# The recurrence's elementwise tiles, made pair by pair in the projections of a hybrid decoder layer and kept in HBM

## The chip, the core and the metric

The kernel runs on one core of a Trainium2 chip. TensorE (PE) multiplies matrices, VectorE (DVE), ScalarE (ACT) and GpSimd (POOL) work elementwise, SyncE (SP) issues most of the DMAs and ACT a few. Each engine works through its own instructions in the order in which the program lists them. The metric is the device time of one execution in microseconds (us).

## The reference

One inference step of a two-layer decoder for a prompt of 1024 tokens and eight samples of eight tokens, model width 1024. Each layer is a mixer, a cross-attention over 256 memory tokens and a squared-ReLU MLP. The mixer of layer 0 is a convolution module, that of layer 1 is RWKV-7 time mixing, which is what changes here:

```python
xr, xw, xk, xv, xa, xg = (h + xx * mix[i] for i in range(6))
r, k, v = xr @ w_r, xk @ w_k, xv @ w_v
w_pre = w0 + tanh(xw @ w1) @ w2
decay = exp(-exp(-softplus(-w_pre) - 0.5))
a = sigmoid(a0 + (xa @ a1) @ a2)
g = sigmoid(xg @ g1) @ g2
kk = k * k_k;  kk = kk / max(sqrt(sum(kk * kk)), 1e-12)      # per head of 64
k = k * (1 + (a - 1) * k_a)
# per token:  s = s * decay + (s @ -kk) (kk * a)^T + v k^T ;  y = s @ r
y = standardize(y) * lnx_g + lnx_b
bonus = sum(r * k * r_k) * v                                  # per head
out = ((y + bonus) * g) @ w_o
```

## The kernel before

Everything is kept channel by token: 128 channels on the partitions, eight blocks of channels (a block holds two heads of 64, so it is a pair of heads; `m` counts the blocks). The tokens are cut into two parts, and each part has a stream of its own: stream A works on part 0 (512 tokens), stream B on part 1 (512 tokens and the 64 sample tokens). Tiles of A have an A in their names (`A_d`, `hAA`, `xA`), those of B a B.

Each stream runs the same stages: convolution, attention, MLP, then in layer 1 the projections (`projections`), the recurrence (`scan`), its output product (`mixer_out`), attention, MLP. A function `pace` takes steps from the two streams in turn, by costs that the steps yield, and stream B's recurrence waits for A's. A list scheduler then fixes the order of every engine's instructions when the program is built. So while A is in its recurrence, what else PE can do is what the order places there of stream B, and the reverse.

Large products are made of three fp32r matmuls for each pair of 128 rows (L142 to L144, in `prod`; the rounded operand and its rest are made by `split`, L96 and L97).

`projections` makes r, k, v (`project`, 24 weight tiles) and the low-rank w, a and g (`hidden`, `lora`) and writes them with `store` into `scr`, one array in HBM for each block, with six slots. `scan` goes over chunks of 64 tokens: eight of part 0, and for part 1 the sample tokens and eight chunks. Its steps for a chunk are generators that `together` runs side by side for three neighbouring chunks:

- `prep` loads the chunk of all eight blocks from `scr` (16 DMAs, L1151), makes the running decay sum (L1171), its exponentials, the scaled r, k, kk and kk*a (L1166 to L1203), the norms of kk with four matmuls (L1208), and the bonus term (L1256 to L1258), all on tiles of 128x512, and between them the products of the chunk (L1224 to L1253);
- `invert` inverts the chunk's triangular matrices of 64x64, mostly on DVE (L1276 to L1322, then PE and DVE in turn);
- `step` carries the state S from chunk to chunk (L1381 to L1408), `step_samples` does the samples;
- `finish` normalizes y and applies lnx_g, lnx_b, the bonus and g on POOL (L1467 to L1471).

The MLP's square on POOL is L711, the time mixing's interpolations are L782 and L783, the attention's spill to HBM is `xa`, and `low` keeps the low halves of the projection weights between the two parts.

## Time and profile before

| | |
|---|---|
| runs of the kernel, us | 3828.97, 3836.46, 3836.49 (median 3836.46) |
| the profiled execution: its time, us | 3837.42 |
| its span, first to last instruction, us | 3835.7 |
| PE busy, us | 3623.9 (94% of the span) |
| DVE busy, us | 2351.6 (61%) |
| ACT, POOL busy, us | 1610.0 (42%), 660.7 (17%) |
| mean granted clock of PE | 0.955 |
| DMA, mean | 119 GB/s |

The span leaves out 1.7 us of the profiled execution's time. Busy shares are means over stages that differ, so the prediction reads them stretch by stretch. The granted clock is a mean over a stretch of PE's two levels, 2.4 GHz (1.00) and 1.2 GHz (0.50).

### The profile page before, as it was taken

What the parts mean: (1) busy time and instruction counts of PE and PEld (TensorE: products, weight loads), DVE (VectorE), ACT (ScalarE), POOL (GpSimd) and SP (SyncE); (2) the same over time, 40 slices, a digit from 0 to 9 for tenths busy, and PEclk for the clock granted to TensorE, in tenths of its full rate; (3) what the DMA queues carried; (4) which work ended last, traced back from release to release, by engine and by line L of the source; (5) the groups of instructions that cost most, each with busy time, mean ns of one, the idle gap of its engine ahead of it and who ended that gap; (6) DMA issues with size and microseconds to landing.
All of it is one profiled execution on the core that took longest, in us unless ns stands there. A gap on an engine that the chain in (4) does not pass through costs nothing.

```text
span 3835.7 us, 75763 instructions
## 1 busy us (share of the span) xinstructions
PE 3623.9 (94%) x30906; PEld 3369.6 (88%) x30906; DVE 2351.6 (61%) x4479; ACT 1610.0 (42%) x3190; POOL 660.7 (17%) x704
## 2 busy tenths in 40 slices
PE   8989979999999999999979998879999999989998
PEld 7767769999999999998768898758799999989998
DVE  7889974646545554437896444778955546553334
ACT  3223253435433354544555654444543435332222
POOL 0010031114201100002332000243330025101110
PEclk9999989999999999999979998889899999989998
DMA  6414223335422344544333784432233336322222
GB/s 226 132 53 129 80 67 106 102 114 170 153 90 83 126 151 152 159 138 112 85 88 109 232 254 146 111 93 70 54 113 120 114 120 197 121 72 83 83 83 64
DMA packets 333004, 456.03 MB, mean 119 GB/s; under 512 B 155248, under 2 KB 247664, under 8 KB 332656
## 3 DMA queue, kind: packets, MB, share of 16 engines
q1 hardware_dynamic: 305008, 424.43, 36.4%
q10 hardware_dynamic: 27648, 26.75, 2.0%
q8 instruction: 243, 3.98, 0.4%
q14 instruction: 105, 0.86, 0.1%
HBM read 369.11 MB, written 73.49 MB: 115 GB/s over the span
## 4 chain that ended last, share of the span: by engine, by line
PE 77%; DVE 11%; ACT 4%; DMA 4%; issue 2%; POOL 1%; SPq 1%; ACTq 0%; DVEq 0%; POOLq 0%
PE B_d L142 11%; PE B_d L144 11%; PE B_d L143 11%; PE A_d L142 10%; PE A_d L143 9%; PE A_d L144 9%; PE A_d L362 3%; PE B_d L362 2%; DMA scr<-t_st 1%; SPq L1151 1%; PE A_hd L810 1%; PE A_d L442 1%; PE B_sa L608 1%; DVE wt L97 1%; PE B_sa L610 1%
## 5 line engine op out<-in xcount | busy, mean ns | idle before, releaser
L97 DVE TENSOR_TENSOR wt<-raw,wt 128x1024 fp32r<-128x1024 f32 x447 | 567.3, 1272 | 476.9 <-ACT wt L96 473.0
L96 ACT CAST wt<-raw 128x1024 fp32r<-128x1024 f32 x488 | 508.5, 1047 | 502.2 <-PE B_d L144 268.6
L142 PE MATMUL B_d<-hAB,wt 128*128 128x288 f32 (+1 forms) x2240 | 673.6, 303 | 15.4 <-ACT hAB L96 6.3
L143 PE MATMUL B_d<-hBB,wt 128*128 128x288 f32 (+1 forms) x2240 | 668.5, 299 | 1.2 <-DVE hBB L97 1.1
L144 PE MATMUL B_d<-hAB,wt 128*128 128x288 f32 (+1 forms) x2240 | 666.2, 298 | 0.3 <-DVE wt L97 0.3
L142 PE MATMUL A_d<-hAA,wt 128*128 128x256 f32 x2240 | 639.1, 288 | 15.0 <-ACT hAA L96 13.6
L143 PE MATMUL A_d<-hBA,wt 128*128 128x256 f32 x2240 | 642.4, 288 | 3.4 <-DVE hBA L97 3.4
L144 PE MATMUL A_d<-hAA,wt 128*128 128x256 f32 x2240 | 632.8, 285 | 2.5 <-POOL wt L97 2.2
L142 PEld LDWEIGHTS A_d<-hAA,wt 128*128 128x128 f32 x2240 | 429.0, 192 | 25.1 <-ACT hAA L96 16.8
L142 PEld LDWEIGHTS B_d<-hAB,wt 128*128 128x128 f32 x2240 | 425.4, 191 | 24.5 <-ACT hAB L96 7.5
L143 PEld LDWEIGHTS A_d<-hBA,wt 128*128 128x128 f32 x2240 | 430.2, 192 | 14.3 <-DVE hBA L97 5.6
L144 PEld LDWEIGHTS A_d<-hAA,wt 128*128 128x128 f32 x2240 | 428.6, 192 | 7.3 <-POOL wt L97 2.6
L143 PEld LDWEIGHTS B_d<-hBB,wt 128*128 128x128 f32 x2240 | 427.2, 191 | 6.5 <-DVE hBB L97 3.7
L711 POOL TENSOR_TENSOR t_sg<-t_ev 128x256 f32<-128x256 f32 (+1 forms) x256 | 185.5, 725 | 1418.2 <-ACT t_ev L709 1329.3
L144 PEld LDWEIGHTS B_d<-hAB,wt 128*128 128x128 f32 x2240 | 426.1, 190 | 2.3 <-issue 0.7
L142 PE MATMUL B_d<-u,wt 128*128 128x288 f32 x1024 | 307.1, 301 | 0.0
L144 PE MATMUL B_d<-u,wt 128*128 128x288 f32 x1024 | 303.3, 299 | 0.0
L143 PE MATMUL B_d<-u,wt 128*128 128x288 f32 x1024 | 303.3, 298 | 0.0
L143 PE MATMUL A_d<-u,wt 128*128 128x256 f32 x1024 | 288.2, 282 | 0.0
L144 PE MATMUL A_d<-u,wt 128*128 128x256 f32 x1024 | 288.2, 282 | 0.0
L142 PE MATMUL A_d<-u,wt 128*128 128x256 f32 x1024 | 287.4, 282 | 0.0
L97 DVE TENSOR_TENSOR u<-t_sg,u 128x256 fp32r<-128x256 f32 (+1 forms) x256 | 130.4, 510 | 149.9 <-ACT u L96 149.6
(401 smaller groups left out, 7068.8 us busy)
## 6 DMA issues: line engine op xcount, KB each, us to landing
raw<-in_mlp_up_dram SPq DMA_DIRECT2D x128, 512.0 KB, 3.6
raw<-in_mlp_dn_dram SPq DMA_DIRECT2D x128, 512.0 KB, 3.6
raw<-in_rw_w_dram SPq DMA_DIRECT2D x64, 512.0 KB, 4.2
ld<-scr SPq DMA_DIRECT2D x136, 128.0 KB, 3.2
wf<-in_w_in_dram SPq DMA_DIRECT2D x32, 512.0 KB, 4.0
raw<-in_xa_w_q_dram SPq DMA_DIRECT2D x32, 512.0 KB, 3.6
raw<-in_xa_w_o_dram SPq DMA_DIRECT2D x32, 512.0 KB, 3.6
raw<-in_ck_dram SPq DMA_DIRECT2D x32, 512.0 KB, 3.6
```

The source lines that it names most:

```text
L96: self.nc.scalar.copy(hi, src)
L97: (engine or self.nc.vector).tensor_tensor(lo, src, hi.bitcast(F32), SUB)
L142: self.nc.tensor.matmul(out, lhsT=wh, rhs=mh, start=(i == 0), stop=False)
L143: self.nc.tensor.matmul(out, lhsT=wh, rhs=ml, start=False, stop=False)
L144: self.nc.tensor.matmul(out, lhsT=wl, rhs=mh, start=False, stop=(i == last))
L362: nc.tensor.matmul(ps[:, :n], lhsT=wt[:, 0, k * P:k * P + P], rhs=h[:, k, t0:t0 + n], start=(k == 0), stop=(k == NC8 - 1))
L442: nc.tensor.matmul(ps[hs], lhsT=dg[:, q, h], rhs=two[h][:, 2 * q:2 * q + 512], start=(q == 0), stop=(q == pairs - 1))
L608: nc.tensor.matmul(out[:, h2], lhsT=wt.rearrange("p i t -> p (i t)"), rhs=moving[:, 0], start=start, stop=stop)
L610: nc.tensor.matmul(out[:64, h2], lhsT=wt[:, 0], rhs=moving[:, 1], start=False, stop=False)
L711: nc.gpsimd.tensor_mul(sg[:, :n], r[:, :n], r[:, :n])
L810: nc.tensor.matmul(ps[:, :n], lhsT=w1[:, m:m + P], rhs=hc[:, :n], start=(c == 0), stop=(c == NC8 - 1))
L1151: nc.sync.dma_start(out=dst[..., m * 64:m * 64 + 64], in_=scr[part][m][:, slots, t0:t0 + 64])
```

## The change

Most elementwise work of `prep` and `finish` goes into a new generator `staged` in `projections`. It works through the eight blocks, and each block in pieces of tokens: two of 256 in part 0 (16 pieces in all), three of 192 in part 1 (24 pieces). For a piece it loads the six slots of `scr` into one tile `ld` (it has one buffer), `stage` computes on it, in place, and the seven results are written to a new array `tls` in HBM; the next piece's load goes into the same `ld`. The squared norms and the chunk-end decays are kept in SBUF (`sums`, `ends`).

`prep` now loads four ready tiles and v, and copies the norms; `finish` loads two ready tiles, multiplies once and adds once. The recurrence's inversions, products and state step are as before. The `a` path's `hidden` moves to the first projection and its `lora` beside the third, and a block's pieces are issued in the third projection once its inputs are there, the last blocks behind it.

```diff
+    tls = [[dram.tile([P, 7, n], F32, name=f"tls{i}_{m}") for m in range(NC8)] for i, (_, n, _) in enumerate(PARTS)]
+    sums = [const.tile([P, NC8, n], F32, name=f"sums{i}") for i, n in enumerate((8, 9))]
+    ends = [const.tile([P, NC8, n], F32, name=f"ends{i}") for i, n in enumerate((8, 16))]
...
+        half, pieces = (192, (0, 3, 6)) if part else (256, (0, 4))
+        ld = hp.tile([P, 7, half], F32, name="ld")
...
+        def stage(m, c0):
+            nch = half // 64
+            tail_in = c0 + nch > 8
+            e_runs = cuts[1:] if tail_in else cuts[:1]
+            w, r, ag, k, v, g, bo = (ld[:, i] for i in range(7))
+            nc.scalar.activation(kk, k, AF.Copy, scale=col("k_k", m))
+            nc.scalar.activation(t1, k, AF.Square, scale=col("k_k", m))
+            ps = s.bank()
+            for i in range(nch):
+                for hs in (slice(0, 64), slice(64, P)):
+                    nc.tensor.matmul(ps[hs, i:i + 1], lhsT=t1[hs, 64 * i:64 * i + 64], rhs=bones[hs, hs][:, :1],
+                                     start=True, stop=True)
+            nc.vector.tensor_scalar_max(sums[part][:, m, c0:c0 + nch], ps[:, :nch], L2_MIN)
+            nc.vector.tensor_tensor_scan(out=w, data0=last_rst if tail_in else rst, data1=w, initial=0.0, op0=MUL, op1=ADD)
+            for e, l in zip(e_runs, runs(w, c0)):
+                nc.scalar.activation(e[:, :, 1:], l, AF.Exp, scale=-DECAY)
+            nc.scalar.activation(w, w, AF.Exp, scale=DECAY)
+            yield .3
+            nc.scalar.activation(t1, ag, AF.Identity, scale=col("k_a", m), bias=less[:, m:m + 1])
+            nc.vector.scalar_tensor_tensor(out=ag, in0=kk, scalar=-1.0, in1=ag, op0=MUL, op1=MUL)
+            nc.vector.scalar_tensor_tensor(out=t1, in0=t1, scalar=1.0, in1=k, op0=ADD, op1=MUL)
+            nc.vector.scalar_tensor_tensor(out=bo, in0=r, scalar=col("r_k", m), in1=t1, op0=MUL, op1=MUL)
+            nc.gpsimd.tensor_tensor(ag, ag, w, MUL)
+            nc.gpsimd.tensor_tensor(k, t1, w, MUL)
+            for i, (e, l, x1, x2, x3) in enumerate(zip(e_runs, (64, DSEQ), runs(r, c0), runs(kk, c0), runs(w, c0))):
+                e0, e1 = (8, 16) if i else (c0, min(8, c0 + nch))
+                nc.gpsimd.tensor_copy(ends[part][:, m, e0:e1], e[:, :, l])
+                nc.gpsimd.tensor_tensor(x1, x1, e[:, :, 1:], MUL)
+                nc.vector.tensor_tensor(x3, x2, e[:, :, :l], MUL)
+            yield .3
+            ps = s.bank()
+            nc.tensor.matmul(ps[:, :half], lhsT=bones, rhs=bo, start=True, stop=True)
+            nc.vector.tensor_tensor(bo, v, ps[:, :half], MUL)
+            nc.vector.scalar_tensor_tensor(out=bo, in0=bo, scalar=col("lnx_b", m), in1=g, op0=ADD, op1=MUL)
+            nc.scalar.activation(g, g, AF.Copy, scale=col("lnx_g", m))
+            yield .3
+        def staged():
+            old = None
+            for m in range(NC8):
+                yield 0
+                for c0 in pieces:
+                    if old is not None:
+                        nc.sync.dma_start(out=old, in_=ld)
+                    ts = slice(64 * c0, 64 * c0 + half)
+                    nc.sync.dma_start(out=ld[:, :6], in_=scr[part][m][:, :, ts])
+                    yield from stage(m, c0)
+                    old = tls[part][m][:, :, ts]
+            nc.sync.dma_start(out=old, in_=ld)
...
                         s.prod(ps[:, :n], wide(wt, h, tt))
                         t = s.small("st")
                         nc.scalar.copy(t[:, :n], ps[:, :n])
-                        store(t, m, (slot + 1) % 3, t0, n)
+                        store(t, m, (1, 3, 4)[slot], t0, n)
                         yield cost(n)
                         for side in sides:
                             yield next(side, 0)
+                    if slot == 2 and m0 and tt == tiles[-1]:
+                        for _ in range(1 + 3 * len(pieces)):
+                            yield next(tiles_of, 0)
                     if m0 == 6 and after is not None:
                         yield from mix(after, tt)
         for tt in tiles:
             yield from mix(0, tt)
-        yield from project(0, 2, hidden(1, "w", [AF.Tanh]))
-        yield from project(1, 3, hidden(5, "gh", [AF.Sigmoid, AF.Sigmoid]), lora("w", 3))
-        yield from project(2, None, hidden(4, "a", [AF.Copy]), lora("gh", 5))
+        tiles_of = staged()
+        yield from project(0, 2, hidden(1, "w", [AF.Tanh]), hidden(4, "a", [AF.Copy]))
+        yield from project(1, 3, hidden(5, "gh", [AF.Sigmoid, AF.Sigmoid]), lora("w", 0))
+        yield from project(2, None, lora("a", 2), lora("gh", 5))
         s.put()
-        yield from lora("a", 4)
+        yield from tiles_of
...
-BUF = dict(w=5, bon=2, at=2, ar=2, Aq=2, UV=2, AV=2, BK=2, v=2, pcs=3)
+BUF = dict(w=5, ld=3, at=2, Aq=2, UV=2, AV=2, BK=2, v=2, pcs=3)
...
     def load(dst, c, slots):
         part, t0 = (1, 512) if c is None else (c // 8, c % 8 * 64)
         for m in range(NC8):
-            nc.sync.dma_start(out=dst[..., m * 64:m * 64 + 64], in_=scr[part][m][:, slots, t0:t0 + 64])
+            nc.sync.dma_start(out=dst[:, m], in_=tls[part][m][:, slots, t0:t0 + 64])
     def prep(chunk):
         sam = chunk is None
         kind = "_s" if sam else "_p"
-        ld = new([P, 4, 512], "ld")
-        load(ld, chunk, slice(1, 5))
-        r, k, ws, ag = (ld[:, i] for i in range(4))
+        part, n = (1, 8) if sam else (chunk // 8, chunk % 8)
+        ld = new([P, 8, 4, 64], "ld")
+        load(ld, chunk, slice(0, 4))
+        ar, bk = ld[:, :, :2], ld[:, :, 2:]
         v = w512("v")
-        load(v, chunk, 0)
-        ar = new([P, 8, 2, 64], "ar")
-        bk = new([P, 8, 2, 64], "bk")
-        kk = w512()
-        nc.vector.tensor_tensor(v3(kk), v3(k), bvec("k_k"), MUL)
...
-        nc.vector.tensor_tensor_scan(out=L, data0=masks["rst"], data1=ws, initial=0.0, op0=MUL, op1=ADD)
...
-        nc.scalar.activation(En, L, AF.Exp, scale=DECAY)
...
-            nc.gpsimd.tensor_tensor(ar[:, :, 0], v3(kk), E[:, :, :64], MUL)
-        t1 = w512()
-        nc.vector.scalar_tensor_tensor(out=v3(t1), in0=v3(ag), scalar=-1.0, in1=bvec("k_a"), op0=ADD, op1=MUL)
-        bp = ag
-        nc.vector.scalar_tensor_tensor(out=bp, in0=kk, scalar=-1.0, in1=ag, op0=MUL, op1=MUL)
-        nc.gpsimd.tensor_tensor(bk[:, :, 0], v3(bp), v3(En), MUL)
-        km = t1
-        nc.vector.scalar_tensor_tensor(out=km, in0=t1, scalar=1.0, in1=k, op0=ADD, op1=MUL)
-        nc.gpsimd.tensor_tensor(ar[:, :, 1], v3(r), v3(E) if sam else E[:, :, 1:], MUL)
-        nc.gpsimd.tensor_tensor(bk[:, :, 1], v3(km), v3(En), MUL)
-        rk = w512()
-        t = w512()
-        nc.gpsimd.tensor_tensor(v3(t), v3(r), bvec("r_k"), MUL)
-        nc.vector.tensor_tensor(rk, t, km, MUL)
+        load(v3(v), chunk, 4)
+        pcs = ends[part][:, :, 8:] if sam else ends[part][:, :, n]
         yield
-        ss = bank("pp")
-        for q in range(4):
-            nc.tensor.matmul(ss[:, 2 * q:2 * q + 2], lhsT=sq[:, q * P:q * P + P], rhs=bones[:, ::64], start=True, stop=True)
-        d4 = d32[:, :16].rearrange("p (q c i) -> p q c i", c=2, i=2)
-        for cp, ps in heads:
-            for h, hs in heads:
-                nc.vector.tensor_scalar_max(d4[hs, :, cp], ss[ps, h:8:2].unsqueeze(2).broadcast_to([64, 4, 2]), L2_MIN)
+        d4 = d32[:, :16].rearrange("p (c i) -> p c i", i=2)
+        nc.vector.tensor_copy(d4, sums[part][:, :, n].unsqueeze(2).broadcast_to([P, 8, 2]))
...
-        sb = bank("pp")
-        nc.tensor.matmul(sb, lhsT=bones, rhs=rk, start=True, stop=True)
-        bon = w512("bon")
-        nc.vector.tensor_tensor(bon, v, sb, MUL)
-        return dict(chunk=chunk, ar=ar, at=at, Aq=Aq, UV=UV, AV=AV, BK=BK, bon=bon, pcs=pcs)
+        return dict(chunk=chunk, ar=ar, at=at, Aq=Aq, UV=UV, AV=AV, BK=BK, pcs=pcs)
...
-        gg = w512("gg")
-        load(gg, chunk, 5)
+        gb = new([P, 8, 2, 64], "gb")
+        load(gb, chunk, slice(5, 7))
         nc.gpsimd.tensor_mul(y, y, rs)
-        nc.gpsimd.tensor_tensor(v3(y), v3(y), bvec("lnx_g"), MUL)
-        nc.gpsimd.tensor_tensor(v3(y), v3(y), bvec("lnx_b"), ADD)
-        nc.gpsimd.tensor_add(y, y, w["bon"])
-        nc.gpsimd.tensor_mul(y, y, gg)
+        nc.gpsimd.tensor_mul(v3(y), v3(y), gb[:, :, 0])
+        nc.gpsimd.tensor_add(v3(y), v3(y), gb[:, :, 1])
```

Three places show what the order of the instructions becomes. The first is PE where part 0's projections end and its recurrence starts. Before, the recurrence's first rows (L1208 is the norms of a chunk, L1381 its state step) stand between stream B's MLP products (`B_d<-u,wt`):

```order
L143 MATMUL B_d<-u,wt 128x288
L1208 MATMUL p_pp<-c_bones,w 128x2 x4
L144 MATMUL B_d<-u,wt 128x288
L142 MATMUL B_d<-u,wt 128x288
L143 MATMUL B_d<-u,wt 128x288
L144 MATMUL B_d<-u,wt 128x288
L143 MATMUL B_d<-u,wt 128x288
L144 MATMUL B_d<-u,wt 128x288
L1381 MATMUL p_pz<-S,ar 64x64 x16
```

Now the pieces stand there. L912 is the eight small norm matmuls of a piece, L934 its bonus sum; the rows ahead of them are the norm of stream B's layer 1, the last of B's rows for a while. This is where piece 10 of the 16 begins:

```order
L260 MATMUL B_d<-c_ident,nv 128x128 x2
L260 MATMUL B_d<-c_ident,nv 128x32
L912 MATMUL A_d<-c_bones,t_12809 64x1 x8
L934 MATMUL A_d<-ld,c_bones 128x256
L912 MATMUL A_d<-c_bones,t_12809 64x1 x8
```

The same two rows follow each other seven times, for pieces 10 to 16, and this is where they end (L1261 is the first product of the recurrence, the next L142 the first projection product of stream B):

```order
L912 MATMUL A_d<-c_bones,t_12809 64x1 x8
L934 MATMUL A_d<-ld,c_bones 128x256
L1261 MATMUL p_pp<-ld 128x128 x2
L1414 MATMUL p_pz<-S,ld 64x64 x2
L142 MATMUL B_d<-hAB,wt 128x288 x2
```

Between the norm matmuls of neighbouring pieces 1 to 10 of part 0, 99 to 282 other matmuls stand in PE's order; between those of pieces 10 to 16 there is none. Of the 23 gaps between part 1's 24 pieces, fifteen hold 96 to 208 matmuls, and the other eight hold 12, 86, 74, 36, 56, 75, 87 and 64.

The second place is DVE at the same point. Before, stream B's projections begin (`rest`, the first DVE row of `projections` for part 1) in the middle of part 0's recurrence, between rows of a state step (L1408) and of the output (L1456):

```order
L1407 TENSOR_TENSOR S<-p_pz,S 128x512
L1322 STREAM_TRANSPOSE T_20125<-td 128x256
L1408 TENSOR_TENSOR S<-S,pcs 128x512
L725 TENSOR_TENSOR xB_169<-xB_169,B_d 128x288
L769 TENSOR_SCALAR rest<-vec 128x48
L1456 SCALAR_TENSOR_TENSOR y<-p_pz,y 128x512
```

Now that row stands behind the last row of the last piece of part 0 (L937), and with it all of stream B's mixing:

```order
L924 SCALAR_TENSOR_TENSOR ld<-ld,vec,t_12809 128x256
L931 TENSOR_TENSOR ld<-kk,ones 128x256
L935 TENSOR_TENSOR ld<-ld,A_d 128x256
L937 SCALAR_TENSOR_TENSOR ld<-ld,vec 128x256
L1309 STREAM_TRANSPOSE dt<-d_18201 128x32
L773 TENSOR_SCALAR rest<-vec 128x48
```

The third place is PE in the recurrence of part 1. Before, products of stream A (`A_d`) stand between the chunk's rows (L1235 and L1245 are transposes of `prep`, L1333 and L1342 belong to the inversion):

```order
L1333 MATMUL p_half<-td,Y_25567 32x16 x4
L1381 MATMUL p_pz<-S,ar 64x64 x3
L143 MATMUL A_d<-hBA,wt 128x256
L144 MATMUL A_d<-hAA,wt 128x256
L142 MATMUL A_d<-hAA,wt 128x256
```

Now, at the same steps of a chunk, row follows row of the recurrence:

```order
L1366 MATMUL p_half<-td,Y_26634 32x16 x32
L1272 MATMUL p_pp<-c_ident,v 128x128 x4
L1282 MATMUL p_pp<-c_ident,ld 128x128 x4
L1414 MATMUL p_pz<-S,ld 64x64 x10
L1375 MATMUL p_half<-T_29141,at 32x32 x16
L1282 MATMUL p_pp<-c_ident,ld 128x128 x4
L1288 MATMUL p_pp<-UV,Aak 64x64 x10
```

From the first row of the samples' step to the last row of part 1's recurrence, PE's order held 1008 product matmuls of stream A (L142 to L144) and now holds 112; in part 0's recurrence it held 983 of stream B and now holds 768.

## Rows read from the trace of the kernel before

**Rows 1.** The page: span, busy time of each engine, the chain that ended last.

```profile
span 3835.7 us, 75763 instructions
...
PE 3623.9 (94%) x30906; PEld 3369.6 (88%) x30906; DVE 2351.6 (61%) x4479; ACT 1610.0 (42%) x3190; POOL 660.7 (17%) x704
...
PE 77%; DVE 11%; ACT 4%; DMA 4%; issue 2%; POOL 1%; SPq 1%; ACTq 0%; DVEq 0%; POOLq 0%
```

**Rows 2.** Windows: us; busy (count) PE, PEld, DVE, ACT, POOL; PEclk, DMA, GB/s.

```profile
1340.00:1740.00 400.00, 399.77 (x3080) 396.17 (x3079) 181.25 (x335) 189.45 (x416) 28.61 (x44) 1.00 0.48 150
1740.00:2130.00 390.00, 349.76 (x4661) 300.09 (x4660) 314.93 (x700) 213.90 (x429) 116.85 (x105) 0.89 0.37 99
2130.00:2300.00 170.00, 159.73 (x1069) 147.57 (x1068) 64.88 (x132) 96.60 (x201) 6.21 (x5) 1.00 0.79 251
2300.00:2860.00 560.00, 505.70 (x6057) 435.03 (x6057) 408.08 (x855) 260.72 (x534) 162.67 (x133) 0.88 0.34 93
2500.00:2600.00 100.00, 78.80 (x871) 58.89 (x870) 84.25 (x175) 47.16 (x100) 45.25 (x34) 0.86 0.30 80
```

**Rows 3.** DMA issues of the whole kernel: count, size, median us to landing.

```profile
raw<-in_mlp_up_dram SPq DMA_DIRECT2D x128, 512.0 KB, 3.6
...
low<-wt SPq DMA_DIRECT2D x24, 512.0 KB, 3.0
...
xa<-xA SPq DMA_DIRECT2D x4, 1024.0 KB, 5.1
...
xA<-xa SPq DMA_DIRECT2D x4, 1024.0 KB, 6.1
...
xA<-xs SPq DMA_DIRECT2D x2, 1024.0 KB, 9.0
...
ld<-scr SPq DMA_DIRECT2D x136, 128.0 KB, 3.2
```

**Rows 4.** Groups by line: 256-wide DVE and POOL, table loads, a weight's split.

```profile
L711 POOL TENSOR_TENSOR t_sg<-t_ev 128x256 f32<-128x256 f32 x128 | 94.8, 741 | 591.2 <-ACT t_ev L709 504.0 <-DVE nv L252 77.6 <-DVE nt L235 3.8
...
L783 DVE SCALAR_TENSOR_TENSOR t_dl<-xA,vec,t_dl 128x256 f32<-128x256 f32 x48 | 22.4, 488 | 3.4 <-ACT t_dl L782 3.3
...
L1463 ACT ACT_TABLE_LOAD x17 | 21.8, 1283 | 0.3
...
L97 DVE TENSOR_TENSOR wt<-raw,wt 128x1024 fp32r<-128x1024 f32 x447 | 567.3, 1272 | 476.9 <-ACT wt L96 473.0
```

**Rows 5.** Groups by line: six rows of DVE in a chunk's preparation.

```profile
L1171 DVE TENSOR_TENSOR_SCAN ld<-rst,ld 128x512 f32<-128x512 f32 x17 | 26.8, 1578 | 2.2 <-DMA v<-scr 2.2
...
L1192 DVE SCALAR_TENSOR_TENSOR w<-ld,vec 128x512 f32<-128x512 f32 x17 | 17.4, 1026 | 0.0
...
L1197 DVE SCALAR_TENSOR_TENSOR w<-w,ld 128x512 f32<-128x512 f32 x17 | 15.6, 915 | 0.0
...
L1194 DVE SCALAR_TENSOR_TENSOR ld<-w,ld 128x512 f32<-128x512 f32 x17 | 15.3, 900 | 0.1
...
L1203 DVE TENSOR_TENSOR w<-w 128x512 f32<-128x512 f32 x17 | 13.6, 800 | 0.2 <-PE p_pp L1208 0.2
...
L1258 DVE TENSOR_TENSOR bon<-v,p_pp 128x512 f32<-128x512 f32 x17 | 11.5, 679 | 7.8 <-PE p_pp L1256 7.8
```

**Rows 6.** Groups by line: PE in the recurrence.

```profile
L1381 PE MATMUL p_pz<-S,ar 64*64 64x64 f32 x512 | 25.9, 247 | 1.6 <-ACT rs L1463 1.6
...
L1256 PE MATMUL p_pp<-w,c_bones 128*128 128x512 f32 x34 | 22.8, 757 | 1.4 <-ACT BK L1246 1.4
...
L1208 PE MATMUL p_pp<-c_bones,w 128*128 128x2 f32 x136 | 21.2, 274 | 1.8 <-ACT AV L1253 1.8
```

**Rows 7.** Timeline of DVE: the same step of two neighbouring chunks, part 1.

```profile
2625.60 1.04 DVE L1286 STREAM_TRANSPOSE M<-dgz 128x512 f32<-128x512 f32 x1
...
2662.68 1.08 DVE L1286 STREAM_TRANSPOSE M<-dgz 128x512 f32<-128x512 f32 x1
```

**Rows 8.** One line's instructions: duration in ns, smallest, median, largest.

```profile
L1194 DVE SCALAR_TENSOR_TENSOR ld<-w,ld x17: 654/691/1672, 1749.7 to 2748.2; 128x512 f32<-128x512 f32 x17
```

69 lines of the change are left out of this document (30 added, 39 removed).

## The prediction

> **What bounds the kernel now.** The page comes first: PE is busy for 3623.9 of 3835.7 us, and 77% of the chain that ended last lies on it [rows 1]. So what counts is where PE idles or runs at less than its full clock, and for that I read windows [rows 2]. In part 0's projections (1340 to 1740 us) PE is busy 399.8 of 400 us at clock 1.00: whatever stands beside them is hidden. In part 0's recurrence (1740 to 2130) PE idles 390 - 349.8 = 40 us, and a mean clock of 0.89 takes about 0.11 x 350 = 38 us more: a shortfall of 78 us. In the start of part 1's recurrence and its chunks (2300 to 2860) it is 560 - 505.7 = 54 us of idle time and about 0.12 x 506 = 60 us by the clock, 114 us. The stretch before it (2130 to 2300) idles 10 us. In the middle of part 1's recurrence (2500 to 2600) DVE is busy 84% and PE 79%: the chain of a chunk, mostly DVE with hand-offs to PE and ACT, sets the pace there, and 37.1 us pass from one chunk's step to the next's [rows 7].
>
> The change takes DVE and POOL work out of the two recurrences, where there is 78 + 114 = 192 us to be had at most, and puts it beside the projections. So the question is whether it is hidden there.
>
> **Part 0's tail.** The order says that it is not, for pieces 10 to 16. They stand back to back on PE with nothing between, ahead of the recurrence's first product; behind them, on DVE, stands all of stream B's mixing, so B's next products (the `hAB` row) can't be early either. SP issues load and store in turn into the one buffer `ld`: a store waits for the piece's computing, the next load for that store. So nothing overlaps, and a piece's period is the sum of three parts.
>
> The load is 6 x 256 x 4 x 128 bytes = 768 KB, the store seven slots, 896 KB. A load of 512 KB lands in 3.6 us and one of 1024 KB in 6.1; a store of 512 KB in 3.0 and one of 1024 KB in 5.1 [rows 3]. Halfway for the load, 4.9 us, and three quarters of the way for the store, 4.6. The computing's longest path is the scan (half of 1.578 us [rows 5], 0.8), two exponentials (no 256-wide Exp is in the trace; like the 0.49 us of a 256-wide row [rows 4], 1.0), and POOL's three products of 0.74 us each [rows 4] and a small copy, about 2.8. With 0.9 us for four or five hand-offs (a choice) that is 5.5 us. The period is 4.9 + 4.6 + 5.5 = 15.0 us. From piece 10 to piece 16 that is 6 x 15.0 = 90 us. Then come the last piece's computing behind its norm (3.5), its store (4.6) and the recurrence's first loads and preparation (3.2 us a load [rows 3], and their queue of 16: I take 8). The little that PE does in the tail (56 small products of 0.27 us that partly overlap, and 7 bonus products of under 0.76 [rows 6]) is counted below as added work, and I take 8 us off here. Sum **+98, taken as +100**. Bounds: with 3.6 and 3.0 us for the transfers the period is 12.1, the sum 81; with 9.0 (the slowest transfer of 1024 KB [rows 3]) and 6.1 it is 20.6, the sum 132.
>
> The page "DMA: Bandwidth & Descriptors" of the Trainium skill (section "Anatomy of one DMA") gives a DMA about 2.0 us fixed, and then bytes over 436 GB/s, for DMAs that GpSimd issues. By it, as an estimate, 1024 KB take 4.4 us, where the rows show 5.1 and 6.1, so the rows decide; its load and store would be 3.8 and 4.1 us, the period 13.4 and this term some 10 us less. It speaks against the change all the same: a chain through one buffer pays a fixed part twice for each piece.
>
> **Part 0's recurrence.** Each of eight chunks loses these DVE rows: 1578 + 1026 + 915 + 900 + 800 + 679 ns = 5.9 us [rows 5], 47 us in all of the 315 that DVE is busy there [rows 2]; POOL loses four products of about 1.4 us less the copies, and ACT three rows. PE waits there mostly on that chain, and stream B's products, now those of its projections, still fill holes. I take four fifths of the 47: **-38**. Bounds: -10, if the inversions and the state step set the pace anyway, and -70, nearly the whole shortfall of 78.
>
> **Part 1's pieces.** With 192 tokens a piece moves 576 and 672 KB: by the same rows 4.2 and 3.9 us, and 5.4 of computing, 13.5. A projection product takes 399.77 us / 3080 = 0.13 us [rows 2], so a gap of 104 matmuls in PE's order just covers a period. Fifteen gaps hold 96 to 208 and cover it, near enough. The other eight (12, 86, 74, 36, 56, 75, 87, 64, together 490) miss 8 x 104 - 490 = 342 matmuls, 44 us. I take 40 where the window before had 10 idle: +30.
>
> **Part 1's recurrence.** A chunk takes 37.1 us now, and 84% of that DVE is busy, 31.3 us [rows 2, 7]. It loses the 5.9 of rows 5. It also loses cover: stream A's products there fall from 1008 to 112, or by 100 for each of nine chunks, and with them the splitting of about four weights (1.27 us each [rows 4]) and the eviction adds, some 8 us of DVE. 17.4 us of DVE stay, and a chunk can't be faster. If it kept its busy share it would be at 21; with all idle time as before (5.8 us), at 23; and if only the six rows went, at 31. I take 26, since three neighbouring chunks still run side by side but nothing fills between. What PE does of use in it: now 0.79 x 37.1 x clock 0.86 = 25 us at full clock, less 100 x 0.13 = 13, so 12. The shortfall of a chunk is 26 - 12 = 14 us, times nine 126, where it was 114: +12, of which the end of the samples' part and the finish (two POOL products fewer of 1.2 to 1.5 us) may give back 9. With the pieces: **+33**. Bounds: at 21 us a chunk it would be 9 x 5 = 45 less, at 31 as much more; with the pieces fully covered (-10) or not, I keep -20 to +85.
>
> **PE's own work and ACT.** PE drops 136 norm products and 34 halves of bonus sums (21.2 + 22.8 us, [rows 6]), and gains 40 bonus sums of half the width and less and some 270 narrow ones, which overlap as the 64x64 ones do: **-4** (-12 to +8). ACT loads its tables 37 times more, 1.28 us each [rows 4], 47 us on an engine that is busy 189 of 400 us in the projections [rows 2]: hidden there, since the pieces' own chain has room in the long gaps. If it were not, it would add to the period of the pieces that change tables, and that lies within the bounds of the period.
>
> **Sum.** 100 - 38 + 33 - 4 = +91. The sum is made against the profiled execution, 3837.4 us, 1 us above the median of the runs: **3928 us**. With all bounds at one end it is -21 or +215.
>
> **Rivals.**
> - *The recurrences give back more than the tail costs (faster).* The work that leaves them may have delayed more than itself. One line does the same work on the same shape in 654 ns at best and 1672 at worst [rows 8], so DVE is held up by something, and POOL worked beside it. If three quarters of the 192 us go, 144, then 3837 + 100 - 144 - 4 = 3789 us. It decides from 104 us on. For it speaks that spread; against it, that inversions and state step stay, that the cover goes to 112 products, and that the median of that line, 691, is near its best. The page "SBUF — State Buffer" of the Trainium skill (section "Who interferes with whom") says that a DVE instruction with two SBUF inputs and a GpSimd one that reads SBUF lock each other out of a shared port for a whole instruction; the spread fits it, though no row here shows a lock, and in the pieces the same pairs meet again.
> - *Part 1's pieces starve as well (slower still).* If a piece takes 4 us more, as with transfers of 9 us that compete with the weights' (the window 2130 to 2300 moves 251 GB/s at a DMA share of 0.79 [rows 2]), the tail pays 6 x 4 = 24, the eight short gaps 8 x 4 = 32: 3928 + 56 = 3984 us.
> - *It cancels (no change).* PE's work is nearly the same, and if the tail is at its lower bound, 81, and the recurrences give back 77 in all, it stays at 3837. It asks for both recurrences to gain, the second without cover.
>
> **How the numbers follow.** Two runs of this kernel differ by up to 0.2% (3828.97 and 3836.49), so less than 0.2% can't be told from no change. The tail is in the order and its period rests on rows that are close, so the forecast, slower by 25 to 165 us, has 0.68; starving pieces 0.15; the gain 0.11; cancelling 0.06. That gives faster 0.11, same 0.06, slower 0.83. For 8 in 10 the range leaves out the gain and a little above: 3862 (tail 85, recurrences -60 together) to 4000 (starving, and the last 16 us of the tail's upper bound).
>
> **What would show it.** The tail: right if at the end of part 0's projections PE is nearly idle for about 90 us, with loads and stores in turn every 15 us; wrong if some product of stream B runs there, or the period is under 12. The recurrences: right if part 0's shortfall is about 40 us, and a chunk of part 1 takes some 26 us with PE idle half of it; wrong if a chunk takes over 31 or under 21. The pieces of part 1: right if PE waits at the norm of the eight with short gaps, and not of the others. The forecast falls if the recurrences give back more than 100 us together, or if PE waits in the long gaps too.

## The result, and the profile after

The changed kernel takes 4174.4 us (median of four runs, 4167.95 to 4183.58) against 3836.5: 338 us slower, ratio 1.0885 (1.0857 to 1.0912). The forecast was 3928, so the direction was right and the size missed by 246 us. The page after, with the rows that answer to [rows 1]:

```profile
span 4170.2 us, 77208 instructions
...
PE 3742.2 (90%) x31360; PEld 3452.6 (83%) x31360; DVE 2336.5 (56%) x4637; ACT 1726.0 (41%) x3424; POOL 579.8 (14%) x747
...
PE 66%; DMA 12%; DVE 10%; ACT 7%; issue 4%; POOL 1%; SPq 1%; ACTq 0%; DVEq 0%; POOLq 0%
```

PE's share of the chain that ended last fell from 77 to 66%, and DMA's rose from 4 to 12%. The windows show where. They follow the stages of [rows 2]; part 0's projections now stand in two rows, with the seven last pieces in the second (columns as in [rows 2]):

```profile
1340.00:1850.00 510.00, 495.45 (x3830) 487.08 (x3828) 254.62 (x483) 251.88 (x523) 64.67 (x90) 0.99 0.51 165
1850.00:2000.00 150.00, 43.75 (x329) 32.98 (x330) 64.09 (x159) 38.24 (x84) 20.56 (x40) 0.55 0.41 121
2000.00:2350.00 350.00, 318.56 (x4193) 265.18 (x4192) 210.06 (x536) 213.97 (x437) 31.38 (x26) 0.87 0.42 116
2350.00:2900.00 550.00, 451.31 (x3385) 423.20 (x3385) 259.45 (x566) 251.68 (x524) 81.02 (x147) 0.89 0.54 169
2900.00:3300.00 400.00, 327.81 (x4397) 257.19 (x4396) 212.30 (x512) 152.03 (x301) 51.30 (x48) 0.72 0.34 86
```

For each stage I add PE's idle time and what the clock takes, (1 - clock) x busy time, as the prediction did; in part 1, where the forecast gave one term of +33, its two parts stand apart:

| stage | shortfall before, us | after, us | more | forecast |
|---|---|---|---|---|
| part 0's projections | 0 | 20 | +20 | 0 |
| its last pieces | - | 106 + 20 = 126 | +126 | +100 |
| part 0's recurrence | 78 | 31 + 41 = 73 | -5 | -38 |
| part 1's projections | 10 | 99 + 50 = 148 | +138 | +30 |
| part 1's recurrence | 115 | 72 + 92 = 164 | +49 | +3 |

These make 328 of the 338 us. The second row of the windows is the tail, with PE busy 44 of 150 us at a clock of 0.55. The timeline there shows one piece, from the scan when its load has landed to the next piece's scan (start, duration, engine, line, what ended the idle time before):

```profile
1891.64 0.69 DVE L916 TENSOR_TENSOR_SCAN ld<-rst,ld 128x256 f32<-128x256 f32 x1 [9.80 <-DMA ld<-scr]
...
1891.70 0.51 ACT L907 ACTIVATE kk<-ld,vec 128x256 f32<-128x256 f32 x1 [9.32 <-DMA ld<-scr]
...
1892.12 0.49 ACT L908 ACTIVATE t<-ld,vec 128x256 f32<-128x256 f32 x1
...
1892.66 1.02 PE L912 MATMUL A_d<-c_bones,t 64*64 64x1 f32 x16 [11.90 <-ACT t L908]
...
1893.73 0.60 ACT L921 ACTIVATE t<-ld,less,vec 128x256 f32<-128x256 f32 x1 [0.36 <-PE A_d L912]
...
1894.36 0.42 DVE L922 SCALAR_TENSOR_TENSOR ld<-kk,ld 128x256 f32<-128x256 f32 x1 [0.47 <-ACT t L921]
...
1894.87 0.84 POOL L925 TENSOR_TENSOR ld<-ld 128x256 f32<-128x256 f32 x1 [1.70 <-DVE ld L922]
...
1895.23 0.75 DVE L924 SCALAR_TENSOR_TENSOR ld<-ld,vec,t 128x256 f32<-128x256 f32 x1
...
1895.66 0.91 POOL L926 TENSOR_TENSOR ld<-t,ld 128x256 f32<-128x256 f32 x1
...
1896.04 1.22 PE L934 MATMUL A_d<-ld,c_bones 128*128 128x256 f32 x2 [2.36 <-DVE ld L924]
...
1896.60 0.88 DVE L931 TENSOR_TENSOR ld<-kk,ones 128x256 f32<-128x256 f32 x1 [0.62 <-POOL ld L926]
...
1897.41 0.41 DVE L935 TENSOR_TENSOR ld<-ld,A_d 128x256 f32<-128x256 f32 x1
...
1897.85 0.48 DVE L937 SCALAR_TENSOR_TENSOR ld<-ld,vec 128x256 f32<-128x256 f32 x1
...
1898.37 0.51 ACT L938 ACTIVATE ld<-ld,vec 128x256 f32<-128x256 f32 x1 [4.05 <-DVE ld L937]
...
1898.94 0.51 SPq L948 DMA_DIRECT2D tls<-ld  x1
...
1903.27 0.57 SPq L950 DMA_DIRECT2D ld<-scr  x1
...
1908.18 0.69 DVE L916 TENSOR_TENSOR_SCAN ld<-rst,ld 128x256 f32<-128x256 f32 x1 [9.84 <-DMA ld<-scr]
```

The computing takes 7.3 us (1891.64 to the store's issue at 1898.94), the store's turn 4.3 and the load's 4.9: 16.5 us a piece. ACT and DVE stand still for over nine of them in one stretch, and PE for about 14 (11.9 before the norms, 2.4 before the bonus sum). The transfers landed in medians near what the forecast took from [rows 3]:

```profile
tls<-ld SPq DMA_DIRECT2D x24, 672.0 KB, 4.5
...
tls<-ld SPq DMA_DIRECT2D x16, 896.0 KB, 4.7
...
ld<-scr SPq DMA_DIRECT2D x24, 576.0 KB, 4.7
...
ld<-scr SPq DMA_DIRECT2D x16, 768.0 KB, 4.9
```

In part 1 a piece with hardly any products beside it shows the period of its own chain. The second gap of the 23 has 12 products:

```profile
2432.01 0.56 DVE L916 TENSOR_TENSOR_SCAN ld<-rst,ld 128x192 f32<-128x192 f32 x1 [3.77 <-DMA ld<-scr]
...
2433.15 1.28 ACT L918 ACT_TABLE_LOAD   x1
...
2435.23 0.53 ACT L921 ACTIVATE t<-ld,less,vec 128x192 f32<-128x192 f32 x1
...
2439.54 0.56 SPq L948 DMA_DIRECT2D tls<-ld  x1
...
2443.65 0.53 SPq L950 DMA_DIRECT2D ld<-scr  x1
...
2448.11 0.56 DVE L916 TENSOR_TENSOR_SCAN ld<-last_rst,ld 128x192 f32<-128x192 f32 x1 [2.90 <-DMA ld<-scr]
```

That is 7.5 us of computing, 4.1 for the store's turn and 4.5 for the load's, 16.1 in all, where the forecast had 13.5. In the other gaps it is longer, and not only where products fill them. These windows run from a piece's norms to the next one's: the gap with 12 products, the sixth, a long one in which PE idles 9.5 us all the same, and the fifteenth, which its own products fill (columns as in [rows 2]):

```profile
2432.90:2449.00 16.10, 5.60 (x26) 4.07 (x26) 4.89 (x12) 5.66 (x14) 1.99 (x4) 0.50 0.63 206
2513.50:2541.50 28.00, 18.55 (x132) 16.40 (x132) 16.51 (x52) 16.79 (x37) 3.55 (x7) 0.88 0.69 222
2719.80:2737.70 17.90, 17.68 (x158) 17.47 (x158) 8.94 (x20) 6.31 (x15) 2.23 (x6) 1.00 0.41 131
```

Over all 23 gaps, cut in this way, PE idles 97 us: 56 in the eight short ones and 41 in the fifteen that the forecast took as covered. Only a third of it stands before the pieces' own rows on PE (L912 and L934, 34 us by the view of PE's waits); the rest stands before products of either stream that wait for ACT or DVE. The two largest rows of that view, between 2350 and 2900 us (total us, times, longest):

```profile
PE B_d L912 <- ACT t L908: 22.7, 13, 7.0
PE A_d L563 <- DVE e L556: 17.3, 7, 5.2
```

ACT and DVE stop too. Their longest waits for a transfer in the same stretch are for the pieces' loads:

```profile
ACT kk L907 <- DMA ld<-scr: 85.1, 24, 6.6
```

```profile
DVE ld L916 <- DMA ld<-scr: 74.3, 23, 9.9
```

Each engine works in order, so while ACT stands at a piece's first instruction, what stands behind it waits as well. How much of PE's idle time comes from that is not shown: the wait of the weights' lower halves for ACT's upper halves (L97 for L96), where it would be looked for, is 473 us over the whole kernel before [rows 4] and 467 after. SP stands still as well. It issues the weights' loads in the same queue as the pieces' transfers, and in this stretch its two longest waits are for a piece's last row, before the store, and for that store's landing, before the next load:

```profile
SPq L948 <- ACT ld L938: 80.5, 22, 12.8
SPq L950 <- DMA tls<-ld: 72.3, 23, 5.6
```

Other loads stand behind these in the queue. No run here issues the pieces' transfers from another engine, so what this costs is open.

Part 1's recurrence, the rows that answer to [rows 7], and the windows over the same chunks:

```profile
3073.57 1.04 DVE L1319 STREAM_TRANSPOSE M<-dgz 128x512 f32<-128x512 f32 x1 [0.42 <-ACT dgz L1306]
...
3104.82 1.05 DVE L1319 STREAM_TRANSPOSE M<-dgz 128x512 f32<-128x512 f32 x1 [2.06 <-ACT dgz L1306]
...
3139.65 1.04 DVE L1319 STREAM_TRANSPOSE M<-dgz 128x512 f32<-128x512 f32 x1
```

```profile
3050.00:3100.00 50.00, 41.97 (x605) 33.45 (x602) 31.86 (x88) 16.59 (x35) 3.80 (x3) 0.62 0.26 59
3100.00:3150.00 50.00, 44.29 (x627) 32.43 (x626) 24.12 (x61) 25.62 (x50) 7.61 (x6) 0.62 0.29 65
3150.00:3200.00 50.00, 46.20 (x636) 37.48 (x634) 30.03 (x81) 18.22 (x38) 3.81 (x3) 0.56 0.23 51
```

A chunk takes 31 and 35 us here, and 23 to 37 over the six steps from 3020 to 3212 us, 32 on average, not 26. The 37.1 us of [rows 7] were the shortest of the six such steps from 2545 to 2790 us, which took 40.8 on average. PE is busy 84 to 92% of the time, but at a granted clock of 0.56 to 0.62, where [rows 2] have 0.86 to 0.88 with products of stream A between.

### The profile page after: what moved, and what is told of

It reads as the page before. It is cut to its first block, busy times and chain, and to the rows that moved or that the text cites. A ratio compares the mean times of both kernels' runs of the same rounds, so it can differ in the third digit from the quotient of the medians.

```text
span 4170.2 us, 77208 instructions
## 1 busy us (share of the span) xinstructions
PE 3742.2 (90%) x31360; PEld 3452.6 (83%) x31360; DVE 2336.5 (56%) x4637; ACT 1726.0 (41%) x3424; POOL 579.8 (14%) x747
## 4 chain that ended last, share of the span: by engine, by line
PE 66%; DMA 12%; DVE 10%; ACT 7%; issue 4%; POOL 1%; SPq 1%; ACTq 0%; DVEq 0%; POOLq 0%
PE B_d L142 9%; PE B_d L143 9%; PE B_d L144 9%; PE A_d L142 7%; PE A_d L143 7%; PE A_d L144 7%; DMA ld<-scr 4%; DMA tls<-ld 4%; PE A_d L367 2%; PE B_d L367 2%; PE p_pp L1261 1%; ACT wt L96 1%; DVE wt L97 1%; DMA scr<-t_st 1%; PE B_hd L814 1%
## 5 line engine op out<-in xcount | busy, mean ns | idle before, releaser
L97 DVE TENSOR_TENSOR wt<-raw,wt 128x1024 fp32r<-128x1024 f32 x447 | 560.8, 1257 | 473.3 <-ACT wt L96 467.1
L96 ACT CAST wt<-raw 128x1024 fp32r<-128x1024 f32 x488 | 508.3, 1046 | 493.6 <-PE B_d L144 232.8
L142 PE MATMUL B_d<-hAB,wt 128*128 128x288 f32 (+1 forms) x2240 | 679.4, 305 | 34.3 <-ACT hAB L96 25.4
L142 PE MATMUL A_d<-hAA,wt 128*128 128x256 f32 x2240 | 639.6, 288 | 44.7 <-ACT hAA L96 21.4
L144 PE MATMUL B_d<-hAB,wt 128*128 128x288 f32 (+1 forms) x2240 | 668.2, 299 | 0.3 <-DVE wt L97 0.3
L144 PE MATMUL A_d<-hAA,wt 128*128 128x256 f32 x2240 | 628.6, 284 | 2.8 <-POOL wt L97 1.9
L142 PEld LDWEIGHTS A_d<-hAA,wt 128*128 128x128 f32 x2240 | 428.5, 192 | 57.0 <-ACT hAA L96 26.0
L142 PEld LDWEIGHTS B_d<-hAB,wt 128*128 128x128 f32 x2240 | 428.6, 192 | 45.1 <-ACT hAB L96 29.0
L144 PEld LDWEIGHTS A_d<-hAA,wt 128*128 128x128 f32 x2240 | 426.4, 191 | 6.1 <-POOL wt L97 2.4
L144 PEld LDWEIGHTS B_d<-hAB,wt 128*128 128x128 f32 x2240 | 428.9, 192 | 2.1 <-DVE wt L97 0.7
L142 PE MATMUL B_d<-u,wt 128*128 128x288 f32 x1024 | 303.2, 298 | 2.1 <-ACT u L96 2.1
L144 PE MATMUL B_d<-u,wt 128*128 128x288 f32 x1024 | 301.0, 296 | 0.4 <-DVE wt L97 0.4
L142 PE MATMUL A_d<-u,wt 128*128 128x256 f32 x1024 | 288.1, 283 | 2.1 <-ACT wt L96 2.1
L144 PE MATMUL A_d<-u,wt 128*128 128x256 f32 x1024 | 288.1, 283 | 0.0
L97 DVE TENSOR_TENSOR u<-t_sg,u 128x256 fp32r<-128x256 f32 (+1 forms) x256 | 130.5, 511 | 143.8 <-ACT u L96 143.5
```

The costliest lines, as they stand in the source:

```text
L96: self.nc.scalar.copy(hi, src)
L97: (engine or self.nc.vector).tensor_tensor(lo, src, hi.bitcast(F32), SUB)
L142: self.nc.tensor.matmul(out, lhsT=wh, rhs=mh, start=(i == 0), stop=False)
L144: self.nc.tensor.matmul(out, lhsT=wl, rhs=mh, start=False, stop=(i == last))
```

## The experiments

Each difference below is against runs of the kernel before that were taken beside it (median 3833 to 3838 us). The diffs are shortened to the lines that matter. Kernels that do only a part of the pieces' work read their data from `scr` in the recurrence, scaled small, and so compute something else.

**The two halves of the change.** `no_pieces` leaves out the pieces, `eng_only` and `dma_only` keep one kind of their work, `two_ld` gives the whole computation a second tile in part 0, and issues a piece's load while the one before is computed; `kk`, `t1` and `rst` move to tiles that are free.

```diff
 no_pieces:  def staged():
+                return
 eng_only:   (the three dma_start lines of staged removed)
 dma_only:  -    yield from stage(m, c0)
            +    for _ in range(3): yield .3
 two_ld:    +    ld = hp.tile([P, 7, half], F32, tag="ld", bufs=1 if part else 2)
```

> The pieces are left out whole (no loads, computing or stores of them; the recurrence loads the raw slots, and the projections' results are scaled to stay small), so this is the recurrence's half of the change alone, 338 us being the whole. Theory A (the time is lost in the pieces, by a chain through one buffer that keeps PE, ACT and DVE waiting): 3800 to 3870 us. Theory B (the recurrence itself got slower, since it lost the products that stood between its rows): 3890 us or more.

> The pieces' computing on all engines stays, in the same steps, on a tile of zeros; their loads and stores are left out, and the recurrence loads the raw slots. Theory A (waits for loads and stores): within 50 us of the kernel without pieces. Theory C (the pieces' own work on ACT, DVE, POOL and PE is what the projections can't hide): most of the 338 us stays, 4050 us or more.

> The pieces' loads and stores through the one tile stay, their computing is left out. Theory A in the form that ACT and DVE stop at the head of their queues until a piece is loaded: no engine waits for a piece any more, so only the start of the recurrence is late, by the seven last pieces at some 9.5 us each; 40 to 90 us above the kernel without pieces. If the DMAs themselves hinder other transfers: 150 us or more above it. Theory C: within 20 us of it.

> The whole computation, with two tiles ld in part 0 (loads are issued a piece ahead within a block, and throughout once the projections' products are issued; kk, t1 and rst use tiles that are free by then). Theory A: a period in the tail falls from 16.5 us to 8 to 11, so the tail loses 40 to 60 us: 4115 to 4140 us, with part 1 as it was. Theory C: no change, 4160 to 4185.

Measured: no_pieces 3769.9 us, 68 less than before (0.9821, 0.9789 to 0.9852); eng_only 3870.6 (+33); dma_only 3879.9 (+42); two_ld 4084.8 (+247). So the loss is in the pieces (A, against B), and it isn't the sum of their parts: over no_pieces, computing adds 101 us, transfers 110, both in one chain 405. Neither part alone meets a range of theory A: eng_only is 51 us above its upper bound, and dma_only 20 above its own. A second tile in part 0 alone takes 90 us off, more than the 40 to 60 expected.

**By part, and by order.** `two_both` has two tiles in both parts, in the way of two_ld; `part0` has pieces for part 0 only; `eng_nope` is eng_only without the norm and bonus sums on PE; `order_only` is the kernel before with the a path moved as in the change.

```diff
 two_both:  +    ld = hp.tile([P, 7, half], F32, tag="ld", bufs=2)
 part0:     +    if part not in (0,): return          # in staged; part 1 uses the old prep
 eng_nope:  -    nc.tensor.matmul(ps[hs, i:i + 1], ...)
            -    nc.tensor.matmul(ps[:, :half], lhsT=bones, rhs=bo, ...)
 order_only: before, with
            +    project(0, 2, hidden(1, "w", ..), hidden(4, "a", ..)); project(2, None, lora("a", 2), lora("gh", 5))
```

> The whole computation, with two tiles ld in both parts. In PE's order the gaps between part 1's pieces get shorter, and 1079 products of stream A stand in part 1's recurrence again, where the changed kernel has 112 and the one with two tiles in part 0 alone 179. Theory A (waits for loads and stores through one buffer, and the cover that part 1's recurrence lost by them): 3890 to 3960 us, toward the 3870 of the kernel without the pieces' DMAs. Theory D (DMA traffic itself, which two buffers don't lessen): 4030 us or more.

> The pieces for part 0 alone; part 1's recurrence prepares its chunks itself, as in the kernel before. From the windows of the changed kernel, part 0's side costs 176 us in the projections and gives back 20 in its recurrence: theory A expects 3960 to 4000 us. Theory E (part 1's loss comes from part 0 being late, not from its own pieces): 4080 us or more.

> The pieces' computing without loads and stores, as before, and without PE's norm and bonus sums and what reads them from PSUM. PE's own time in these is 47 us by the profile of the kernel with computing alone (3870 us). Theory F (its 101 us over the kernel without pieces are PE's own work and the clock behind it): 3800 to 3830 us. Theory C (ACT's and DVE's work holds up the projections): 3850 us or more.

> The kernel before with the a path moved as the change moves it (its hidden layer beside the first projection, its lora beside the third) and the slots of scr renumbered, no pieces. All theories: within 10 us of the kernel before, 3828 to 3848 us; if the moved path is itself worth something, that belongs to the 68 us of the kernel without pieces.

Measured: two_both 3975.8 (+139), part0 3974.2 (+138), eng_nope 3900.1 (+64), order_only 3853.3 (+17; 1.0049, 1.0032 to 1.0066). The second tile is worth 198 of the 338 us, though 16 us less than theory A's range asked. Part 0 costs 138, and so, by subtraction, part 1 the other 200; E falls. The surprise is eng_nope: with less work than eng_only it is 29 us slower, and order_only, which changes no amount of work, costs 17, where every theory allowed 10. F falls. C's figure is met, but less work that takes longer can't be the work's amount: the order that the scheduler writes moves the time by such amounts by itself. The windows of two_both (part 0's projections, its recurrence, part 1's projections, its recurrence):

```profile
1340.00:1917.00 577.00, 543.37 (x4216) 527.79 (x4219) 316.14 (x647) 297.54 (x619) 84.52 (x128) 0.95 0.57 178
1917.00:2229.00 312.00, 296.74 (x3968) 247.39 (x3964) 186.08 (x492) 188.41 (x389) 27.27 (x22) 0.88 0.43 118
2229.00:2721.00 492.00, 400.39 (x3005) 364.34 (x3005) 250.58 (x573) 237.99 (x512) 73.05 (x134) 0.82 0.60 188
2721.00:3034.00 313.00, 303.38 (x4326) 254.28 (x4320) 212.57 (x492) 149.90 (x297) 54.43 (x49) 0.87 0.33 84
```

Against the changed kernel the tail and part 1's recurrence are mostly mended (shortfalls 61 and 49 us for 1340 to 1917 and 2721 to 3034); part 1's projections are not: 92 us idle and 72 by the clock.

**Cover and pacing.** `cost2` and `offset60` change one number of the pacing in the changed kernel, `two_best` combines several on two_both, `scan_evict` moves one DVE row of the kernel before.

```diff
 cost2:      -            yield .3          (in stage, three times)
             +            yield 2.0
 offset60:   -OFFSET = 5.0
             +OFFSET = 60.0
 two_best:   two_both, with yield 1.5 and
             +    for _ in range((2 if m0 == 2 else 1) * (1 + 3 * len(pieces))):
 scan_evict: before, with, in lora("w") at eviction
             +    nc.vector.tensor_tensor_scan(out=t[:, :n], data0=rp or rq, data1=t[:, :n], ...)
             -    nc.vector.tensor_tensor_scan(out=L, data0=masks["rst"], data1=ws, ...)   (in prep)
```

> The changed kernel with one number changed: a step of a piece costs 2.0 instead of 0.3 in the pacing of the two streams, so that stream A advances less while part 1's pieces wait. PE's order then holds 845 products of stream A in part 1's recurrence where the changed kernel holds 112; the seven bare pieces of part 0 and the one buffer stay. Theory G (the products that are missing there cost the recurrence its clock and its cover, some 50 us of shortfall, and 25 behind it): 4085 to 4125 us. Rival H (the products are only taken from between the pieces, where PE then waits instead): 4155 us or more.

> The changed kernel with one number changed: stream B starts its attention 60 instead of 5 behind in the pacing, so that some of its MLP is left when part 0's last pieces come. Of the six bare gaps in PE's order three stay (0, 0, 0 and 24, 125, 142 for the others). Theory A for the tail (each bare period costs what it lasts, 16.5 us): 45 to 60 us less, 4110 to 4130 us. Rival H (B's work that fills the tail is missing in the stretches after it): 4155 us or more.

> Both at once with two tiles ld in both parts (3976 us), two blocks' pieces issued at the first place, and a step's cost at 1.5. The order holds 1301 products in part 1's recurrence and no bare gap in part 0. Theory A: 3920 to 3965 us, between the kernel with computing alone (3870) and 3976; a change below 3836 would need the pieces' computing to cost less than it did alone, which no theory here expects.

> The kernel before with one of the six DVE rows moved: the running decay sum is made where w leaves PSUM (32 scans of 256 columns in part 0's and 24 of 256 or 64 in part 1's projections), on the tile that is there anyway, with no load or store added; 17 rows of 1.58 us go from the recurrence. Theory I (what the recurrence gives back comes from DVE rows on its chain, and such a row is free beside the projections if nothing is loaded for it): 10 to 25 us faster, 3811 to 3826. Rival J (the recurrence gives back only when the whole preparation goes): within 8 us of the kernel before.

Measured: cost2 4158.0 (16 us less than the changed kernel), offset60 4149.7 (25 less), two_best 3998.8 (23 more than two_both, and 34 above theory A's range), scan_evict 3844.7 (+7; 1.0025, 1.0013 to 1.0037). Theory G falls: with 845 products back in part 1's recurrence only 16 us are gained, as rival H says. By the windows the shortfall of part 1's recurrence falls by 51 us in cost2, from 124 to 73 (2969.1 to 3246.1 after, 2950.9 to 3265.0 in cost2), and that of all that follows it rises by 31. So a bare stretch that is filled leaves a hole elsewhere: the products that PE can do beside the chain are a fixed store. offset60 lies between both. scan_evict agrees with J: a row of 1.58 us taken off each chunk, and nothing gained.

**The chain's length, its traffic, its work.** `short_chain` takes one wait out of a piece's chain; the others run one kind of the pieces' work on two tiles.

```diff
 short_chain: -   nc.scalar.activation(t1, k, AF.Square, ...)    lhsT=t1[hs, ...]
              +   nc.scalar.activation(bo, k, AF.Square, ...)    lhsT=bo[hs, ...]
 dma_two:     two_both without stage;   eng_two: two_both without the pieces' dma_start
```

> The changed kernel, whole; only the square for the norms is written into the slot bo instead of t1, so that the scaling of a (L921) no longer waits until PE has read t1. Nothing else is taken out. Theory K (the time goes with how long a piece's chain from load to store takes, over 40 pieces in a row): some 1.5 us less in a period that nothing else sets, 30 to 60 us less in all, 4115 to 4145 us. Theory C (the amount of work): 4165 us or more.

> Loads and stores of the pieces alone, as in the run with DMAs alone (3880 us), but through two tiles in both parts; a memset of slot 6 on POOL for each piece. The same bytes move in about half the time in a row. Theory K: 3770 to 3805 us, near the kernel without pieces (3770). Theory D (the traffic hinders other transfers): 3865 us or more.

> The pieces' computing alone, as in the run with computing alone (3870 us), but on two tiles of zeros in turn, so that a piece need not wait for the end of the one before in all its steps (kk and t1 are still shared). Theory K: 3800 to 3845 us. Theory C (the work itself on ACT, DVE, POOL and PE): 3860 us or more.

Measured: short_chain 4139.7, 35 us less than the changed kernel, with all its work, as theory K asks. Its period in the tail, by the rows of the same engines:

```profile
1927.79 0.69 DVE L916 TENSOR_TENSOR_SCAN ld<-rst,ld 128x256 f32<-128x256 f32 x1 [9.93 <-DMA ld<-scr]
...
1928.59 0.58 ACT L921 ACTIVATE t<-ld,less,vec 128x256 f32<-128x256 f32 x1
...
1928.73 0.93 PEld L912 LDWEIGHTS A_d<-c_bones,ld 64*64 64x64 f32 x16 [12.68 <-ACT ld L908]
...
1943.18 0.69 DVE L916 TENSOR_TENSOR_SCAN ld<-rst,ld 128x256 f32<-128x256 f32 x1 [9.82 <-DMA ld<-scr]
```

L921 no longer waits for PE's norm products, and the period is 1943.18 - 1927.79 = 15.4 us, 1.1 less. Over 40 pieces that is 44 us, if it counted in each; where products fill a gap it need not, and 35 us are within what an order alone has moved here, so the total by itself doesn't show K. But dma_two 3871.3 (+34) and eng_two 3863.1 (+25) gain only some 8 us each by halving a chain of one kind, no more than their runs differ among themselves, as D and C ask. So each half alone has some 100 us over no_pieces that don't go with its length.

> The kernel without pieces (3770 us), but with the pieces' steps kept in the pacing of the two streams (the empty steps cost 0.3 each, 120 of them), nothing done in them. Theory L (the loss of about 100 us that each half of the pieces' work showed alone comes from the order that the pacing then writes, whatever stands in the steps): 3850 to 3885 us. Theory M (it comes from the work that stands there, DMAs in one run, computing in the other): 3760 to 3790 us.

> Loads and stores alone through two tiles (3871 us), with the steps at no cost in the pacing. Theory L: 3765 to 3800 us. Theory M: 3855 us or more.

> The whole computation with two tiles ld in both parts (3976 us), with the steps at no cost in the pacing. Theory L: about 100 us less, 3870 to 3910 us. Theory M: 3960 to 3995 us.

```diff
 pace_only:  def staged():       (no_pieces, with empty steps)
 +               for m in range(NC8):
 +                   yield 0
 +                   for c0 in pieces:
 +                       for _ in range(3): yield .3
 dma_two_free, two_both_free:  - yield .3   + yield 0
```

Measured: pace_only 3848.4 (+15), dma_two_free 3839.5 (+6), two_both_free 3984.2 (+151). Empty steps alone cost 78 of those 100 us: the same work as no_pieces, in another order. In part 0's recurrence (no_pieces first, then pace_only; columns as in [rows 2]) the same chunks take 266 us at a clock of 0.89 or 357 at 0.81, with 208 more matmuls beside them:

```profile
1744.00:2010.00 266.00, 249.36 (x3850) 210.38 (x3850) 184.74 (x459) 138.62 (x279) 40.88 (x48) 0.89 0.35 91
```

```profile
1755.00:2112.00 357.00, 340.50 (x4058) 278.52 (x4058) 201.26 (x514) 164.40 (x331) 38.20 (x45) 0.81 0.32 87
```

So theory L is right for pace_only (it ends 2 us below its range). dma_two_free lies between L and M: the free steps give back about 30 us of its loss, and over no_pieces, which has the same free steps, its transfers still cost 70. The 78 us are therefore no fixed share of the 100. For the whole work M is right: two_both_free gains nothing.

## Why the prediction was right and wrong

With pace_only (+15 against before) as the base with the same steps, the parts read: computing alone 10 to 18 us more, transfers alone 19 to 27, both through two tiles 124, both through one tile 323. With no_pieces (-68) as the base with free steps, transfers alone read some 70 and both through two tiles some 215, so each part is known only to the some 80 us that an order is worth. The whole through one tile is beyond that: most of what is lost is lost where load, computing and store stand in one row.

Against the table of stages every term of the forecast missed on the same side, and together they make 233 of the 246 us, so nothing in the sum came right by luck.

- **Part 0's tail**: right in place and kind. The period was 16.5 us for 15.0: the transfers 9.2 for 9.5, the computing 7.3 for 5.5. The forecast's longest path was the scan, two exponentials and POOL. The real one begins with ACT's square (L908) and PE's norms (L912), for which L921 waits, since it overwrites `t1`; it goes on over L922, POOL's products (L925, L926) and DVE's L931, which waits for them, and ends with two more rows of DVE and one of ACT (L935, L937, L938). The bonus sum (L934) is done 0.15 us before L935 starts, and isn't what it waits for. 126 us for 100: 9 of it is the period, 20 the clock, which the forecast had left out of this term.
- **Part 1's pieces**: this is the step that failed most, +138 for +30. "Fifteen gaps hold 96 to 208 and cover it, near enough" took a matmul that stands in PE's order as 0.13 us of cover, at full clock, against a period of 13.5. All three failed. The period of a bare piece is 16.1: the transfers 8.6 for 8.1 (by a straight line between the rows that the forecast names they would be 3.9 and 3.7, not 4.2 and 3.9), the computing 7.5 for 5.4; L921 stands here behind a table load and other rows of ACT. With 16.1 a gap needs 124 matmuls, the eight short ones then miss 502, 65 us, and the windows show 56 where 44 were forecast; that is the mis-sized part. The fifteen others idle 41 us where the forecast had none, most of it before products whose operands come late from ACT or DVE: standing in the order doesn't make a product ready. And the clock takes 50 us (0.89 in the stretch), which the sum had at nothing. The rival of starving pieces had the longer piece, but looked for it in the transfers (9 us instead of 4.7), priced it at 56 us in all, and left the long gaps covered too.
- **Part 0's recurrence**: forecast -38, measured -5, or -20 if the windows are cut closer to it (70 us from 1794.3 to 2100.8 before, 50 from 2002.8 to 2313.4 after). In these closer windows DVE is busy 183 us instead of 246, and the stretch takes 311 us for 307, so it is no faster for it. scan_evict agrees on the kernel before: a DVE row taken off the chunks gave nothing, though its order is another too. How much the recurrence's half is worth stays open: -68 us in one order (no_pieces), +15 in another (pace_only), with equal work. The step that reads a saving on DVE as time is the one that is not borne out.
- **Part 1's recurrence**: the chunk came out at 32 us for 26, above the 31 that the prediction named as a sign of being wrong, and PE is not idle half of it. The lost cover was seen, but a chunk was priced by DVE's work and hand-offs at full clock, while PE fell to a clock of about 0.6 and became the busy engine. Putting the cover back (cost2) moved the loss instead of ending it.
- **PE's own work and ACT**: eng_only, eng_two and eng_nope put the computing at 10 to 49 us over pace_only, without a clear share for PE. The -4 isn't tested by them finely enough. ACT's table loads rose from 56 to 93 by the traces, the 37 that were forecast; what they cost by themselves isn't separated. They are not all hidden: in the bare piece of part 1 shown above one of 1.28 us stands in the chain.
- **The rivals.** The faster one fell: even free of pieces the recurrence gave back 68 us in the better of the orders tried, and it needed 104. Cancelling fell with it.

The page "DMA: Bandwidth & Descriptors" of the Trainium skill (section "Anatomy of one DMA") has a fit for DMAs that GpSimd issues; by it, as an estimate, part 0's transfers would take 3.8 and 4.1 us. The rows show 4.9 and 4.7, so the rows of before were the better guide, as the prediction had it. The page "Perfetto Trace Analysis" of the Trainium skill says (section "Optimization Strategy") that a gap that repeats for a stretch on the engine that should be saturated can mean too few buffers; the trace agrees, with PE idle for some 14 of every 16.5 us in the tail, and the second tile took 198 us off.

What stays open: why part 1's projections keep a shortfall of 164 us with two tiles (two_both), where SP's two waits at the pieces are still 77 and 65 us between 2229 and 2721 us, and what in an order makes 78 us of difference at equal work. The runs show that it does, in the clock and length of part 0's recurrence above all, not which rows cause it. A part 1 with pieces and a part 0 without was not tried. No version with pieces that does the whole computation beats the kernel before; the nearest, part0 and two_both, lie at +138 and +139 us.

## What to carry to other kernels

A round trip through one buffer costs its whole chain for each round, load, computing and store added up: walk the computing's longest path over every engine, and look for a tile with two uses, before holding it against the work that is to cover it. Count a product as cover only from when its operands are there. Work that covers one stall is taken from another, so price a stage by what all engines still have to do, the clock of a PE that waits included. And where a program's order is made from costs, run the new order with empty steps first: here it moved the time by 78 us before any work stood in it.
